# Memory layer: decay of the old states on ScalarE, norm from undivided sums, signed high parts, and states requested in the gates

## Chip, core and metric

One core of one Trainium2 chip. The metric is the device time of one execution in microseconds (us). The engines by their profile names: PE is TensorE (PEld its weight loads), ACT is ScalarE, DVE is VectorE, POOL is GpSimd, SP is SyncE, which issues all DMAs here.

## The reference, cut to what matters

One inference step of a two-layer decoder for a prompt of 256 tokens and for 8 samples of 8 tokens, 320 tokens in all. Layer 0 mixes tokens by a gated MLP, layer 1 by an mLSTM "matrix memory"; a convolutional feed-forward follows each. The change lies in layer 1. For each of 8 heads it computes

```
C, n, m = carry                                  # the old state, 128 x 256 a head and sample
w_inter = exp(inter - m_t);  w_intra = exp(D - m_t)
sc  = (q @ k.T) * w_intra
num = w_inter * (q @ C) + sc @ v
den = w_inter * (q @ n) + sum(sc)
h   = num / maximum(abs(den), exp(-m_t))
decay = exp(bL + m - m_new);  kg = k * g
C_new = decay * C + kg.T @ v
n_new = decay * n + sum(kg)
hn = (h - mean(h)) * rsqrt(var(h) + EPS) * gn_g
y  = (sigmoid(o_pre) * hn) @ w_out
```

Only the samples have an old state; it is an input and its successor an output. Ahead of the layer stands an RMS norm, whose factor 1/sqrt(mean(x²)+EPS) each token's projections are multiplied by.

## The kernel before

**Precision by parts.** Each fp32 weight block of 128x1024 (`raw`) is split into a high part `wh`, rounded (ScalarE, L135), and the rest `wl` (VectorE, L136). A block of 128 outputs is 24 matmuls of 320 columns: `wh` with the high and the low part of the input, `wl` with the high part. Blocks are taken in a fixed list; the load (SyncE) runs 4 chunks ahead into 4 `raw` buffers, the split 1 chunk ahead into 3 pairs of `wh`, `wl`. So a split waits until PE has done with the block three before.

**Order.** PE's instructions keep the order of the program text (`pin`). On the other engines and the queues, a planner in the framework lays out the order from estimated costs, the program's order being the priority; each engine then runs its list strictly in order. Every dependence becomes a semaphore.

**Layer 1** (`layer_b`). `gates` computes, for all heads at once, the gate rows; it begins with the projection `pg`, the norm (`norm_cols`: sums over channels by matmuls with ones, then `ms`, and `rc` by a power on GpSimd; `norm_row`: the same factor as a row `rb`), the first head's q, k, v and output-gate blocks, and the transposes `pt`. Then come heads 1 to 7, each in six weight blocks: q, k (`qk_epi`), two of v (`v_epi`), two of the output gate (`o_epi`), and among them, for that head or the one before:

- `scores`: `pMb` (the head's decays and weights, broadcast to 128 rows), `psc` (q against k), the weights `w` by exp, their product `Pf` and its parts `Ph`, `Pl`, `Pr`, `Ps`, and `dec`, the old states' decay.
- `k_nat`, `v_nat`: transposes `pk`, `pv`, and the parts `kz`, `kgh`, `kgl`, `vh`, `vl`.
- `hand_over`: `inter` (q against the old states `C0`, into `num`), `state_sample` (the new contributions, four tiles `pcs`), `state_out` (C0 = C0·dec + pcs, then its DMA) for two of the four tiles; `close`: `state_out` for the other two, `numer` (`num`), `state_prompt` (`pCp`).
- `stats`: mean and variance of `num`, the normaliser, and `hn`; `finish`: its transposes `phn` and the output's parts `yhb`, `ylb`.

The sums of these helpers lie in five one-bank PSUM buffers (`psa`); the blocks have three of their own (`psm`). The samples' tokens stand twice in a 128-wide tile (`spread`, `twice`), so that one row carries a high part and its twin the low part of the same product; `mk`'s columns are masks for that.

`state_in` requests a head's four `C0` tiles (258 KB each); there are 8 buffers, from the pool `hp`, which opens when the gates' rows are given back.

Of the kernel before, what the change touches and what calls it, by code (L numbers as in the profile page):

```python
# [10 lines left out]
F32 = mybir.dt.float32  # L11
# [5 lines left out]
P = 128  # L17
EPS = 1e-6
TP = 256
NB, NS = 8, 8  # L20
# [17 lines left out]
class Net:  # L38
# [156 lines left out]
    @staticmethod  # L195
    def spread(x):

        return x.rearrange("p (g d s) -> p g d s", g=4, d=2)
# [8 lines left out]

    def norm_cols(self, parts=None, twice=False):
# [5 lines left out]
        if twice:  # L214
            acc2 = self.tp.tile([P, P], F32, tag="acc2", name="acc2", bufs=1)
            nc.vector.tensor_copy(self.spread(acc2), self.twice(self.acc[:, TP:]))
        for t in range(3):
            for i, a in enumerate(parts):
                a_t = acc2 if twice and t == 2 else self.tokens(a, t)
                self.mm(pv[:, t, :], a_t, self.ones[:, :2], i == 0, i == len(parts) - 1)  # L220
# [4 lines left out]
        self.rc, self.rc_twice = rc, twice  # L225

    def norm_row(self):

        nc = self.nc
        dg = self.tp.tile([P, T], F32, tag="sq", name="dg", bufs=2)  # L230
        pb = self.psa.tile([P, 512], F32, tag="pa", name="pb")
        for t in range(2):
            nc.vector.tensor_scalar(dg[:, t * P:(t + 1) * P], self.ident, self.rc[:, t:t + 1], None, op0=MULT)
        if self.rc_twice:
            nc.vector.tensor_scalar(dg[:, TP:].rearrange("p (g s) -> p g s", g=4), self.spread(self.ident)[:, :, 0, :],
                                    self.rc[:, 2:3], None, op0=MULT)
        else:
            nc.vector.tensor_scalar(dg[:, TP:], self.ident[:, 64:], self.rc[:, 2:3], None, op0=MULT)
        self.mm(pb[:, :T], self.ones, dg, True, True)
        rb = self.tp.tile([P, T], F32, tag="rb", name="rb", bufs=1)  # L240
        nc.scalar.copy(rb, pb[:, :T])
        self.rb = rb
# [307 lines left out]
    def layer_b(self):  # L550
# [5 lines left out]
        with ExitStack() as ctx:  # L556
# [4 lines left out]
            nS = lp.tile([P, NH, NB], F32, name="nS")  # L561
            nP = lp.tile([P, NH], F32, name="nP")
# [4 lines left out]
            mk = lp.tile([P, NB + 5], F32, name="mk")  # L567
            mxb = lp.tile([P, 64], F32, name="mxb")
            gm = lp.tile([P, 4, NH], F32, name="gm")
            mo = lp.tile([8, 9], F32, name="mo")  # L570
            mkr = lp.tile([P, NB], F32R, name="mkr")
            pads = []
# [11 lines left out]
            def gates(rp):  # L584
# [126 lines left out]
            def scores(h):  # L711
# [20 lines left out]
                for o in (0, TP):  # L732
# [8 lines left out]

                nc.vector.tensor_scalar(Pr, Pf[:, 384:], mk[:, NB:NB + 1], None, op0=MULT)
                nc.vector.tensor_tensor(spread(Ps)[:, :, 0, :], Pf[:, 384:].rearrange("p (g s) -> p g s", g=4),
                                        Pr.bitcast(F32).rearrange("p (g s) -> p g s", g=4), op=SUB)
                s["P"] = (Ph, Pl, dec)

            def v_nat(h):
# [6 lines left out]
                for t in (2, 0, 1):  # L754
                    dst = dsts[t]
                    sc = self.rc[:, t:t + 1]
                    nc.scalar.activation(vh[:, t, :DV], dst[:, :DV], AF.Copy, scale=sc)
                    nc.vector.scalar_tensor_tensor(vl[:, t, :DV], dst[:, :DV], sc, vh[:, t, :DV].bitcast(F32), op0=MULT, op1=SUB)

            def k_nat(h):  # L760
# [6 lines left out]
                kgl = hp.tile([P, 2, P], F32R, tag="kgl", name="kgl", bufs=1)  # L767
                kr = hp.tile([P, 2, P], F32R, tag="kr", name="kr", bufs=1)
                kz = hp.tile([P, 2, P], F32R, tag="kz", name="kz", bufs=1)
                src = pk[:, 2 * P:3 * P]  # L770

                for i in range(2):
                    nc.vector.tensor_scalar(kr[:, i, :], src, gm[:, 2 + i, h:h + 1], None, op0=MULT)
                    nc.vector.scalar_tensor_tensor(kz[:, i, :], src, gm[:, i, h:h + 1], kr[:, i, :].bitcast(F32), op0=MULT, op1=SUB)
                for t in range(2):
# [6 lines left out]
            def state_in(h):  # L782
                S[h]["C"] = []
                for i in range(4):
                    C0 = hp.tile([P, 2, CW], F32, tag="C0", name="C0", bufs=8)
                    nc.sync.dma_start(C0, I["C0"][h, :, 2 * i:2 * i + 2, :])
                    S[h]["C"].append(C0)

# [20 lines left out]
            def state_out(h, g):  # L809
                s = S[h]  # L810
                dec, C0, pcs = s["P"][2], s["C"][g], s["pcs"][g]
                for u in range(2):
                    b = 2 * g + u
                    nc.vector.scalar_tensor_tensor(C0[:, u, :DV], C0[:, u, :DV], dec[:, b:b + 1], pcs[:, u * DV:(u + 1) * DV],
                                                   op0=MULT, op1=ADD)
                nc.sync.dma_start(O["Cs"][h, :, 2 * g:2 * g + 2, :], C0[:, :, :DV])

# [14 lines left out]
            def stats(h):  # L832
# [13 lines left out]
                nc.vector.tensor_scalar(t1, t1, EPS, None, op0=ADD)  # L846
                sl = hp.tile([P, 3], F32, tag="sl", name="sl", bufs=1)
                nc.gpsimd.tensor_tensor(sl, t1, self.mhalf.to_broadcast([P, 3]), op=ALU.pow)
                nc.vector.tensor_tensor(sl, sl, rd, op=MULT)
                nb = hp.tile([P, 3], F32, tag="nb", name="nb", bufs=1)  # L850
# [4 lines left out]
            def state_prompt(h):  # L855
                s = S[h]
                kgh, kgl, kz = s["kg"]
                dec = s["P"][2]
                pc = self.psa.tile([P, 512], F32, tag="pa", name="pCp")
                for t in range(2):  # L860
                    mm3(pc[:, :CW], kgh[:, t, :], kgl[:, t, :], vh[:, t, :], vl[:, t, :], t == 0, t == 1)
                for i in range(2):
                    mm(pc[:, 264:272], kz[:, i, :], mkr, i == 0, i == 1)
# [78 lines left out]

            state_in(0)
            scores(0)
# [60 lines left out]
            begin(2)  # L1005
            nc.sync.dma_start(O["nP"], nP)
            nc.sync.dma_start(O["nS"], nS)
# [56 lines left out]
def _lay_out(i):  # L1064
# [58 lines left out]
    for h in range(NH):  # L1123
# [3 lines left out]
    tok = s // 32 * 16 + s % 16  # L1127
    low, odd = s // 16 % 2, s // 8 % 2
    a["blk"] = np.concatenate([tok[:, None] // NS == np.arange(NB)[None, :], np.stack(
        [low, 1 - odd, odd, (1 - odd) * low, odd * low], axis=1)], axis=1).astype(f)  # L1130
    a["mxb"] = np.where((tok[:, None] // NS == q[None, :] // NS) & (tok[:, None] <= q[None, :]), f(-1e30), f(1e4))
# [27 lines left out]
```

## Time and profile before

| | |
|---|---|
| median of 3 runs | 970.95 us (970.72 to 971.68) |
| the profiled execution | 970.37 us, of it span 968.6 us |
| busy PE, PEld, DVE, ACT, POOL | 951.8, 922.9, 684.6, 489.8, 75.1 us |
| the memory layer's mixer | 425 to 727 us of the span |
| granted PE clock | 0.996 |

The page gives the busy time of each engine; the waits say for which result an engine stood still, and the timeline lists instructions in order of start, with the number merged in one row behind an x, and in brackets the idle time before the first of them and what ended it. Within a row's name "out<-in" gives tiles. The tile called C is `C0`.

### The profile page before, as it was taken

To read this page: it belongs to the slowest core of one execution; us is meant where nothing else is said; L and a number is where in the kernel's file an instruction comes from. 1 tells how busy PE (TensorE), PEld (TensorE's weight loads), DVE (VectorE), ACT (ScalarE), POOL (GpSimd) and SP (SyncE) were. 2 spreads that over 40 slices of the span, in tenths; PEclk is the share of its full clock that TensorE was granted. 3 is DMA by queue.
4 is the path that set the end of the run, shared out by engine and by line. 5 is a ranking of instruction groups with operands and counts; after the bars stand their busy time and mean duration, and the time that the engine had idled before them with its cause. 6 is when DMAs were issued, how large, how long until landed. Compare 5 with 4: busy or idle time off the path is not lost. (4 is left out here: it accounts for less than half of the span.)

```text
span 968.6 us, 17160 instructions
## 1 busy us (share of the span) xinstructions
PE 951.8 (98%) x6527; PEld 922.9 (95%) x6527; DVE 684.6 (71%) x1333; ACT 489.8 (51%) x851; POOL 75.1 (8%) x248
## 2 busy tenths in 40 slices
PE   9999999999999999999899999999999999999996
PEld 7779999999999999999789999999899999999996
DVE  5757985577777764549889887787787777775442
ACT  6557444444554443447555665464565445454332
POOL 2200000010000000013100001001001000000000
PEclk9999999999999999999999999999999999999998
DMA  7835344434444444453755556544364444445541
GB/s 249 237 130 178 128 138 153 152 131 153 152 153 153 145 152 142 158 174 133 266 182 183 178 181 206 190 152 150 100 216 151 151 145 147 148 149 151 154 123 54
DMA packets 56663, 154.71 MB, mean 160 GB/s; under 512 B 6838, under 2 KB 18486, under 8 KB 56582
## 3 DMA queue, kind: packets, MB, share of 16 engines
q1 hardware_dynamic: 56582, 153.62, 48.4%
q8 instruction: 51, 0.84, 0.4%
q14 instruction: 30, 0.25, 0.1%
HBM read 141.66 MB, written 11.94 MB: 159 GB/s over the span
## 5 line engine op out<-in xcount | busy, mean ns | idle before, releaser
L135 ACT CAST wh<-raw 128x1024 fp32r<-128x1024 f32 (+3 forms) x255 | 257.7, 1011 | 336.6 <-PE pm L47 189.3
L136 DVE TENSOR_TENSOR wl<-raw,wh 128x1024 fp32r<-128x1024 f32 (+3 forms) x255 | 302.0, 1184 | 137.9 <-ACT wh L135 135.6
L47 PE MATMUL pm<-xh,wh 128*128 128x320 f32 x1216 | 379.6, 312 | 0.0
L47 PE MATMUL pm<-xh,wl 128*128 128x320 f32 x1216 | 375.8, 309 | 0.0
L47 PE MATMUL pm<-xl,wh 128*128 128x320 f32 x1216 | 375.7, 309 | 0.0
L47 PEld LDWEIGHTS pm<-xh,wh 128*128 128x128 f32 x1216 | 228.4, 188 | 0.8
L47 PEld LDWEIGHTS pm<-xl,wh 128*128 128x128 f32 x1216 | 228.4, 188 | 0.3
L47 PEld LDWEIGHTS pm<-xh,wl 128*128 128x128 f32 x1216 | 228.2, 188 | 0.0
L47 PE MATMUL pm<-yh_f,wh 128*128 128x320 f32 x352 | 109.0, 310 | 0.0
L47 PE MATMUL pm<-yh_f,wl 128*128 128x320 f32 x352 | 108.5, 308 | 0.0
L47 PE MATMUL pm<-yl_f,wh 128*128 128x320 f32 x352 | 108.5, 308 | 0.0
L47 PEld LDWEIGHTS pm<-yl_f,wh 128*128 128x128 f32 x352 | 66.1, 188 | 0.0
L47 PEld LDWEIGHTS pm<-yh_f,wh 128*128 128x128 f32 x352 | 66.1, 188 | 0.0
L47 PEld LDWEIGHTS pm<-yh_f,wl 128*128 128x128 f32 x352 | 66.1, 188 | 0.0
L472 DVE SCALAR_TENSOR_TENSOR fcv<-fpad,vecs,fcv 128x336 f32<-128x336 f32 x88 | 49.6, 565 | 2.2 <-ACT fcv L470 0.7
L266 DVE TENSOR_TENSOR xT<-pm,xT 128x320 f32<-128x320 f32 x40 | 19.6, 491 | 41.9 <-PE pm L47 41.7
L47 PE MATMUL pm<-yhb,wh 128*128 128x320 f32 x128 | 40.2, 314 | 0.2 <-ACT yhb L891 0.2
L47 PE MATMUL pm<-ylb,wh 128*128 128x320 f32 x128 | 39.6, 309 | 0.4 <-DVE ylb L892 0.4
L47 PE MATMUL pm<-yhb,wl 128*128 128x320 f32 x128 | 39.5, 308 | 0.5 <-DVE wl L136 0.5
L47 PE MATMUL pm<-yh_a,wh 128*128 128x320 f32 x128 | 39.6, 309 | 0.0
L47 PE MATMUL pm<-yh_a,wl 128*128 128x320 f32 x128 | 39.5, 308 | 0.0
L47 PE MATMUL pm<-yl_a,wh 128*128 128x320 f32 x128 | 39.5, 308 | 0.0
(255 smaller groups left out, 1251.3 us busy)
## 6 DMA issues: line engine op xcount, KB each, us to landing
raw<-in_f_up SPq DMA_DIRECT2D x88, 512.0 KB, 3.2
raw<-in_b_win SPq DMA_DIRECT2D x48, 512.0 KB, 3.4
raw<-in_f_dn SPq DMA_DIRECT2D x32, 448.0 KB, 3.2
C<-in_C SPq DMA_DIRECT2D x32, 258.0 KB, 5.1
raw<-in_a_win SPq DMA_DIRECT2D x16, 512.0 KB, 3.2
raw<-in_a_wo SPq DMA_DIRECT2D x16, 512.0 KB, 3.6
raw<-in_f_dn SPq DMA_DIRECT2D x16, 512.0 KB, 3.5
out_Cs<-C SPq DMA_DIRECT2D x32, 256.0 KB, 4.3
```

The costliest lines, as they stand in the source:

```text
L47: self.pin(self.nc.tensor.matmul(out, lhsT, rhs, start=start, stop=stop))
L135: self.last_split = nc.scalar.copy(wh[:, :kn, :], raw[:, :kn, :])
L136: self.last_low = nc.vector.tensor_tensor(wl[:, :kn, :], raw[:, :kn, :], wh[:, :kn, :].bitcast(F32), op=SUB)
L266: self.nc.vector.tensor_tensor(x, ps[:, :T], x, op=ADD)
L472: nc.vector.scalar_tensor_tensor(cv, pd[:, i:i + NC], self.vec(w + i * KF), cv, op0=MULT, op1=ADD)
```

## The change

- `norm_cols` no longer writes the samples' sums out twice before it multiplies them. A new `norm_twice`, behind `norm_row`, makes the doubled copy on ScalarE, and takes one more product and one more power for `v_nat`'s factor `rc2`.
- `dec` is copied by ScalarE, not VectorE, and kept for all heads (`decs`); the update of the normaliser n, two VectorE operations a head, is done once for all heads at the end by GpSimd. ScalarE copies ten columns of `pCp` where it copied one.
- `state_out`: ScalarE multiplies each old state by its decay in place (two instructions a tile), VectorE then adds the tile's `pcs` in one instruction.
- `kz` and `Pr`, `Ps`: the masked rounding is made by ScalarE with a signed mask; VectorE then adds the masked full value (one instruction in place of two).
- `stats`: instead of dividing, the power is taken of var + EPS·d², so three small VectorE steps ahead of it and one behind it go.
- `state_in(0)` moves from behind the gates into them, behind the first q block, and the `C0` buffers move to the layer's own pool `lp`.

```diff
-                self.norm_cols(twice=True)
+                self.norm_cols()
                 p0 = self.block(KD, self.x_rhs)
                 self.norm_row()
+                self.norm_twice()
                 nc.vector.tensor_tensor(zi, gr[:40], self.rb[:40, :], op=MULT)
                 qk_epi(0, 0, p0)
+                state_in(0)
...
+    def norm_twice(self):
+        acc2 = self.tp.tile([P, P], F32, tag="acc2", name="acc2", bufs=1)
+        nc.scalar.copy(self.spread(acc2), self.twice(self.acc[:, TP:]))
+        pc = self.psa.tile([P, 512], F32, tag="pa", name="pc2")
+        self.mm(pc[:, 0:2], acc2, self.ones[:, :2], True, True)
+        ms = self.tp.tile([P, 1], F32, tag="ms2", name="ms2", bufs=1)
+        rc = self.tp.tile([P, 1], F32, tag="rc2", name="rc2", bufs=1)
+        nc.vector.tensor_scalar(ms, pc[:, 0:1], 1.0 / D, EPS, op0=MULT, op1=ADD)
+        nc.gpsimd.tensor_tensor(rc, ms, self.mhalf, op=ALU.pow)
+        self.rc2 = rc
...
-                dec = hp.tile([P, NB], F32, tag="dec", name="dec", bufs=2)
-                nc.vector.tensor_copy(dec, pb[:, 384:392])
+                dec = decs[:, h, :]
+                nc.scalar.copy(dec, pb[:, 384:392])
...
-                nc.vector.tensor_scalar(Pr, Pf[:, 384:], mk[:, NB:NB + 1], None, op0=MULT)
-                nc.vector.tensor_tensor(spread(Ps)[:, :, 0, :], Pf..., Pr..., op=SUB)
+                nc.scalar.activation(Pr, Pf[:, 384:], AF.Copy, scale=mk[:, NB + 5:NB + 6])
+                nc.vector.scalar_tensor_tensor(spread(Ps)[:, :, 0, :], Pf..., mk[:, NB:NB + 1], Pr..., op0=MULT, op1=ADD)
...
                 for i in range(2):
-                    nc.vector.tensor_scalar(kr[:, i, :], src, gm[:, 2 + i, h:h + 1], None, op0=MULT)
-                    nc.vector.scalar_tensor_tensor(kz[:, i, :], src, gm[:, i, h:h + 1], kr[:, i, :].bitcast(F32), op0=MULT, op1=SUB)
+                    nc.scalar.activation(kz[:, i, :], src, AF.Copy, scale=gm[:, i, h:h + 1])
+                    nc.vector.scalar_tensor_tensor(kz[:, i, :], src, gm[:, 2 + i, h:h + 1], kz[:, i, :].bitcast(F32), op0=MULT, op1=ADD)
...
                 for u in range(2):
                     b = 2 * g + u
-                    nc.vector.scalar_tensor_tensor(C0[:, u, :DV], C0[:, u, :DV], dec[:, b:b + 1], pcs[:, u * DV:(u + 1) * DV],
-                                                   op0=MULT, op1=ADD)
+                    nc.scalar.activation(C0[:, u, :DV], C0[:, u, :DV], AF.Copy, scale=dec[:, b:b + 1])
+                nc.vector.tensor_tensor(C0[:, :, :DV], C0[:, :, :DV], pcs.rearrange("p (u v) -> p u v", u=2), op=ADD)
...
                 nc.vector.tensor_tensor(rd, dn, colsT[:, :, 64 + h], op=MAX)
-                nc.vector.reciprocal(rd, rd)
-                t1 = hp.tile([P, 3], F32, tag="t1", name="t1", bufs=1)
-                nc.vector.tensor_tensor(t1, mv[:, :, 1], rd, op=MULT)
-                nc.vector.tensor_tensor(t1, t1, rd, op=MULT)
-                nc.vector.tensor_scalar(t1, t1, EPS, None, op0=ADD)
+                nc.vector.scalar_tensor_tensor(rd, rd, EPS, rd, op0=MULT, op1=MULT)
+                nc.vector.scalar_tensor_tensor(rd, rd, TINY, mv[:, :, 1], op0=MAX, op1=ADD)
                 sl = hp.tile([P, 3], F32, tag="sl", name="sl", bufs=1)
-                nc.gpsimd.tensor_tensor(sl, t1, self.mhalf.to_broadcast([P, 3]), op=ALU.pow)
-                nc.vector.tensor_tensor(sl, sl, rd, op=MULT)
+                nc.gpsimd.tensor_tensor(sl, rd, self.mhalf.to_broadcast([P, 3]), op=ALU.pow)
...
-                nc.scalar.copy(nP[:, h:h + 1], pc[:, DV:DV + 1])
-                nc.vector.tensor_tensor(nS[:, h, :], n0[:, h, :], dec, op=MULT)
-                nc.vector.tensor_tensor(nS[:, h, :], nS[:, h, :], pc[:, 264:272], op=ADD)
+                nc.scalar.copy(nPS[:, h, :], pc[:, DV:DV + 10])
...
+            nc.gpsimd.tensor_tensor(nS, n0, decs, op=MULT)
+            nc.gpsimd.tensor_tensor(nS, nS, nPS[:, :, 2:], op=ADD)
```

More of the change, by code (lines that the diff above doesn't have):

```diff
@@ L18 @@
 EPS = 1e-6
+TINY = 1e-37
 TP = 256
@@ L206, in tokens, with norm_cols @@
         return a[:, (0, P, T - P)[t]:(P, TP, T)[t]]
-    def norm_cols(self, parts=None, twice=False):
+    def norm_cols(self, parts=None):
         nc = self.nc
@@ L213, in norm_cols @@
         pv = pc[:, 0:6].rearrange("p (t e) -> p t e", e=2)
-        if twice:
-            acc2 = self.tp.tile([P, P], F32, tag="acc2", name="acc2", bufs=1)
-            nc.vector.tensor_copy(self.spread(acc2), self.twice(self.acc[:, TP:]))
         for t in range(3):
             for i, a in enumerate(parts):
-                a_t = acc2 if twice and t == 2 else self.tokens(a, t)
-                self.mm(pv[:, t, :], a_t, self.ones[:, :2], i == 0, i == len(parts) - 1)
+                self.mm(pv[:, t, :], self.tokens(a, t), self.ones[:, :2], i == 0, i == len(parts) - 1)
         rc = self.tp.tile([P, 3], F32, tag="rc", name="rc", bufs=2)
@@ L224, in norm_cols @@
         nc.gpsimd.tensor_tensor(rc, ms, self.mhalf.to_broadcast([P, 3]), op=ALU.pow)
-        self.rc, self.rc_twice = rc, twice
+        self.rc = rc
+    def norm_twice(self):
+        nc = self.nc
+        acc2 = self.tp.tile([P, P], F32, tag="acc2", name="acc2", bufs=1)
[7 more added lines that the diff above has]
+        self.rc2 = rc
     def norm_row(self):
@@ L233, in norm_row @@
             nc.vector.tensor_scalar(dg[:, t * P:(t + 1) * P], self.ident, self.rc[:, t:t + 1], None, op0=MULT)
[L234 to L238, printed above, removed]
+        nc.vector.tensor_scalar(dg[:, TP:], self.ident[:, 64:], self.rc[:, 2:3], None, op0=MULT)
         self.mm(pb[:, :T], self.ones, dg, True, True)
@@ L561, in layer_b @@
             nS = lp.tile([P, NH, NB], F32, name="nS")
-            nP = lp.tile([P, NH], F32, name="nP")
             gnh = lp.tile([P, 16], F32, name="gnh")
@@ L566, in layer_b @@
             sel = lp.tile([P, NH, P], F32R, name="sel")
-            mk = lp.tile([P, NB + 5], F32, name="mk")
+            mk = lp.tile([P, NB + 6], F32, name="mk")
             mxb = lp.tile([P, 64], F32, name="mxb")
@@ L570, in layer_b @@
             mo = lp.tile([8, 9], F32, name="mo")
+            decs = lp.tile([P, NH, NB], F32, name="decs")
+            nPS = lp.tile([P, NH, 10], F32, name="nPS")
             mkr = lp.tile([P, NB], F32R, name="mkr")
@@ L755, in v_nat @@
                     dst = dsts[t]
-                    sc = self.rc[:, t:t + 1]
+                    sc = self.rc[:, t:t + 1] if t < 2 else self.rc2
                     nc.scalar.activation(vh[:, t, :DV], dst[:, :DV], AF.Copy, scale=sc)
@@ L767, in k_nat @@
                 kgl = hp.tile([P, 2, P], F32R, tag="kgl", name="kgl", bufs=1)
-                kr = hp.tile([P, 2, P], F32R, tag="kr", name="kr", bufs=1)
                 kz = hp.tile([P, 2, P], F32R, tag="kz", name="kz", bufs=1)
@@ L784, in state_in @@
                 for i in range(4):
-                    C0 = hp.tile([P, 2, CW], F32, tag="C0", name="C0", bufs=8)
+                    C0 = lp.tile([P, 2, CW], F32, tag="C0", name="C0", bufs=8)
                     nc.sync.dma_start(C0, I["C0"][h, :, 2 * i:2 * i + 2, :])
@@ L857, in state_prompt @@
                 kgh, kgl, kz = s["kg"]
-                dec = s["P"][2]
                 pc = self.psa.tile([P, 512], F32, tag="pa", name="pCp")
@@ L941, in close @@
                 state_prompt(h)
-            state_in(0)
             scores(0)
@@ L1128, in _lay_out @@
     low, odd = s // 16 % 2, s // 8 % 2
+    sign = 1 - 2 * low
     a["blk"] = np.concatenate([tok[:, None] // NS == np.arange(NB)[None, :], np.stack(
-        [low, 1 - odd, odd, (1 - odd) * low, odd * low], axis=1)], axis=1).astype(f)
+        [low, (1 - odd) * sign, odd * sign, (1 - odd) * low, odd * low, sign], axis=1)], axis=1).astype(f)
     a["mxb"] = np.where((tok[:, None] // NS == q[None, :] // NS) & (tok[:, None] <= q[None, :]), f(-1e30), f(1e4))
```

9 lines of the change are left out of this document (5 added, 4 removed).

## The prediction

> **What bounds the kernel now.** I read the page first, then the stages, then PE's own waits. All rows in this part and below are of the kernel before.
>
> ```profile
> span 968.6 us, 17160 instructions
> PE 951.8 (98%) x6527; PEld 922.9 (95%) x6527; DVE 684.6 (71%) x1333; ACT 489.8 (51%) x851; POOL 75.1 (8%) x248
> ```
>
> PE is busy for 98% of the span, and the change takes no matmul away. So it can gain only where PE stands still or runs slowly for want of an operand: 16.8 us of the span in all. The table by stage says how much of that lies in the memory layer (columns: stretch, its length, busy us of PE, PEld, DVE, ACT, POOL, granted clock, DMA share, GB/s).
>
> ```profile
> 425.00:727.00 302.00, 294.23 (x2189) 280.91 (x2187) 248.50 (x623) 170.30 (x354) 34.35 (x92) 1.00 0.54 179
> 461.60:490.56 28.96, 24.67 (x192) 20.95 (x191) 25.50 (x70) 15.27 (x37) 4.67 (x7) 1.00 0.66 223
> 490.56:683.00 192.44, 191.37 (x1451) 185.03 (x1452) 158.45 (x406) 106.50 (x227) 17.33 (x51) 1.00 0.53 178
> ```
>
> The layer holds 302.00 − 294.23 = 7.8 us of PE idle time. More than half of it, 4.3 us, lies in the 29 us around heads 0 and 1; heads 2 to 6 (the last row) lose only 1.1 us in 192. VectorE is busy for 82% of the layer and ScalarE for 56%, so the change moves work from the fuller engine to the emptier one, but in the long middle neither holds PE up. The waits of PE name the places (columns: who waited for whom, us in total, times, longest).
>
> ```profile
> PE pcs L47 <- DVE vl L758: 1.4, 1, 1.4
> PE pc L47 <- DVE acc L216: 1.2, 1, 1.2
> PE pk L50 <- ACT w L730: 1.2, 1, 1.2
> ```
>
> ```profile
> PE psc L47 <- ACT kh L274: 1.0, 4, 0.4
> PE phn L50 <- ACT hn L853: 0.8, 1, 0.8
> PE pm L47 <- DVE wl L136: 0.5, 1, 0.5
> PE num L47 <- DMA C<-in_C: 0.5, 1, 0.5
> PE pm L47 <- DVE ylb L892: 0.4, 2, 0.3
> ```
>
> **The change part by part.** The sum is made against the profiled execution, 970.37 us, which is 0.58 us below the median of 970.95.
>
> *Norm.* The timeline of PE at the layer's start, and then at the next norm, which has no doubled sums:
>
> ```profile
> 428.33 0.61 PE L47 MATMUL pc<-ones,acc 128*128 128x2 f32 x4
> 430.19 0.38 PE L47 MATMUL pc<-ones,acc 128*128 128x2 f32 x2 [1.25 <-DVE acc L216]
> 430.43 0.39 PE L47 MATMUL pm<-xh,wh 128*128 128x320 f32 x1
> ```
>
> ```profile
> 726.69 0.72 PE L47 MATMUL pc<-ones,acc 128*128 128x2 f32 x6
> 727.28 0.39 PE L47 MATMUL pm<-xh,wh 128*128 128x320 f32 x1
> ```
>
> Undoubled, the six products pass in 727.28 − 726.69 = 0.59 us, so the block would start at 428.92 and not at 430.43: −1.5. The extra product of `norm_twice` costs a third of 0.59, +0.2, if its copy is done by then; a whole block of matmuls stands between, so I expect no wait. If the planner puts that copy behind the one of the row `rb` on ScalarE, PE waits for both, at most twice this:
>
> ```profile
> L241 ACT COPY rb<-pb 128x320 f32<-128x320 f32 x4 | 1.7, 424 | 0.0
> ```
>
> That would be +0.8. I take −1.5 + 0.2, rounded to −1.2 for a little of that risk; ends −1.5 and −0.4. The new power (`rc2`) takes what POOL's powers take, 0.92 us in a row below, and is first read in `v_nat`, behind the last of the gates' blocks: nothing.
>
> *States requested early.* The first head's 16 products with the old states against the second's:
>
> ```profile
> 462.08 2.82 PE L47 MATMUL num<-C,Qz 128*32 128x258 f32 x16 [0.46 <-DMA C<-in_C]
> 464.82 0.40 PE L47 MATMUL pcs<-vh,kz 32*128 32x256 f32 x4
> ```
>
> ```profile
> 487.80 1.08 PE L47 MATMUL num<-C,Qz 128*32 128x258 f32 x16
> ```
>
> With the tiles there, 2.82 − 1.08 = 1.7 and the wait of 0.46 go: 2.2 us at most. What is late next is the fourth `pcs` buffer, which holds `pk` until its last reader:
>
> ```profile
> 463.05 0.34 DVE L779 SCALAR_TENSOR_TENSOR kgl<-pk,cols,kgh 128x128 fp32r<-128x128 f32 x1
> ```
>
> `pk` is free at 463.4, 1.4 us before `pcs` starts now; VectorE reaches that step earlier by what it is spared, and PE comes earlier by the norm's share. I take half, −1.1 (ends −2.2 and 0). The loads are moved on SP's queue past two or three weight loads; head 1's can follow at once, since all eight buffers are free. The tile's own view gives an issue's length (ns, least, median, most):
>
> ```profile
> L786 SPq DMA_DIRECT2D C<-in_C x32: 327/394/503, 456.9 to 625.4; - x32
> ```
>
> Eight of 0.394 are 3.2 us by which a weight load can come later. Four chunks are loaded ahead, and the chain shows what PE needs for one:
>
> ```profile
> 688.88 3.52 PE pm L47 x24
> ```
>
> So I cost it at nothing. With that cover gone it would be up to 3.2 us, once.
>
> *Old states.* Prices from the groups by form (busy us, mean ns of one):
>
> ```profile
> L814 DVE SCALAR_TENSOR_TENSOR C<-C,dec,pcs 128x256 f32<-128x256 f32 x64 | 26.2, 475 | 0.7 <-PE pcs L47 0.7
> L331 DVE TENSOR_TENSOR vs<-vs,pvs 64x512 f32<-64x512 f32 x4 | 2.8, 692 | 0.1
> L757 ACT ACTIVATE vh<-pv,rc 128x256 fp32r<-128x256 f32 x24 | 11.0, 472 | 3.1 <-DVE vl L758 2.0 <-PE pv L50 1.2
> L773 DVE TENSOR_SCALAR kr<-pk,gm 128x128 fp32r<-128x128 f32 x16 | 5.5, 344 | 0.0
> L742 DVE TENSOR_SCALAR Pr<-Pf,mk 128x64 fp32r<-128x64 f32 x8 | 2.0, 246 | 0.0
> L778 ACT ACTIVATE kgh<-pk,cols 128x128 fp32r<-128x128 f32 x16 | 5.8, 365 | 5.4 <-DVE kz L774 3.3 <-PE pm L47 2.2
> ```
>
> VectorE pays 64·0.475 = 30.4 us now and 32·0.692 = 22.1 after (the sum of two operands of 512 columns, one from PSUM, stands nearest). With 16 `kr` (5.5) and 8 `Pr` (2.0) it sheds 15.8 us, 2 a head, and some seven steps of three to eight columns a head beside. ScalarE's multiplication from SBUF by a column is not in the trace; the nearest row is `vh`, 0.472, of the same size and with the same kind of scale. It gains 64·0.472 + 16·0.365 and the 8 `Pr` at no more than that, 39 us, which makes 209 of 302: no bound. The multiplications wait only for `inter`, not for `pcs`, and this is the gap into which they fall in head 2:
>
> ```profile
> 523.30 1.05 ACT L135 CAST wh<-raw 128x1024 fp32r<-128x1024 f32 x1 [3.67 <-PE pm L47]
> ```
>
> Eight of 0.472 are 3.8 us against 3.67 idle, so the next `wh` is late by 0.1 us, and it is for the block after the next: one block of 3.5 us covers it. If the cover were gone, it would be 0.1 a head.
>
> *Tail and middle.* At the end PE's wait of 0.5 for `wl` follows eight state updates on VectorE; the `ylb` waits of 0.4 follow the same queue; I take −0.8 of these 0.9 (ends −0.9, 0), and −0.5 of the 1.0 for `kh` (ends −1.0, +0.5). The normaliser's two sums on POOL feed nothing but a DMA. Their nearest row is this one:
>
> ```profile
> L848 POOL TENSOR_TENSOR sl<-t,mhalf 128x3 f32<-128x3 f32 x8 | 7.4, 923 | 16.7 <-DVE t L846 16.6
> ```
>
> Two of them make 1.8 us by which SP reaches the weight loads behind that DMA later; the chunks loaded ahead cover it, as above, and without them it is 1.8 once.
>
> *Bank order.* What speaks against the change is in ScalarE's waits:
>
> ```profile
> ACT dn L839 <- DVE bstat L837: 10.4, 17, 1.2
> ```
>
> ```profile
> ACT kgh L778 <- DVE kz L774: 3.3, 3, 1.1
> ```
>
> `dn` needs nothing of `bstat`, nor `kgh` of `kz`; each pair only reads the same PSUM bank, and one engine's reads stand behind the other's. The Trainium skill ("PSUM — Partial Sum Buffer", PSUM bank collisions raise a hardware error) gives the rule: two engines must not touch one bank and quadrant at the same time, not even both to read. By it every added turn is queued, and the sum would be that of the first rival; the trace agrees that turns are kept (the 10.4 us), and not yet that PE pays for them. The change adds such turns: `dec` (ScalarE) ahead of `Qz` and `w` (VectorE) ahead of exp (ScalarE) in `pMb`, and `kz` twice in `pk`. In head 1:
>
> ```profile
> 475.56 0.28 DVE L728 SCALAR_TENSOR_TENSOR w<-pMb,cols,mxb 128x64 f32<-128x64 f32 x1
> 475.75 1.22 DVE L136 TENSOR_TENSOR wl<-raw,wh 128x1024 fp32r<-128x1024 f32 x1
> ```
>
> ```profile
> 476.42 0.76 ACT L730 ACTIVATE w<-pMb,cols 128x256 f32<-128x256 f32 x2
> ```
>
> Now VectorE reads `pMb` at once and ScalarE comes at 476.42. After, `dec` itself takes that place, and if VectorE is then in a `wl`, exp slips by up to 0.3 (`dec`, no longer than the row of `w`) + 1.2 (`wl`) + 0.3 (`w`) = 1.8 us, and PE's wait for `pk` (1.2) with it. Against that, `stats` has four steps fewer and frees `hn` earlier (the 0.8), and VectorE's shorter queue helps `vl` (the 1.4). For head 1 I take −0.6 (ends −2.2 and +1.8), for the same turn in heads 2 to 7 +0.6 (ends 0 and +4).
>
> Sum: −1.2 − 1.1 − 0.8 − 0.5 − 0.6 + 0.6 = −3.6: 966.8 for a profiled execution, 967.3 us as a median.
>
> **Rivals.** *Bank turns decide (slower).* In head 3 the score's bank is given back by `Pf` and PE asks for `pv` here:
>
> ```profile
> 539.79 0.63 DVE L739 SCALAR_TENSOR_TENSOR Pf<-psc,w 128x448 f32<-128x448 f32 x1 [0.17 <-POOL w L733]
> ```
>
> ```profile
> 542.02 0.49 PE L50 MATMUL pv<-ident,vTb 128*128 128x128 f32 x3
> ```
>
> The slack is 542.02 − 540.42 = 1.6 us; a slip of exp by more than that stops PE in each head. At the full 1.8 in head 1 and some 0.6 in each of six heads (0.2 over the slack at `pv`, 0.4 where `kz`'s two turns of 0.34 to 0.37 delay `pk` and `vh`) this is +5.4 against −3.1 from norm, states and tail: about 973.2. That turns are kept the waits of ScalarE show; that PE pays for them no row shows yet. *Next limit close behind.* Norm and tail gain, but at heads 0 and 1 PE meets VectorE's next step in place of the old one: −1.2 − 0.4 and nothing else, 969.4. The full VectorE of that stretch (25.50 of 28.96 us) speaks for it. *All waits go.* The emptier VectorE clears heads 0, 1 and 7 wholly: the good ends, −1.5 − 2.2 − 0.9 − 1.0 − 2.2 = −7.8, or with half of the last three −5.8: 965.2.
>
> **Numbers.** A measurement of this kernel can tell about 0.2%, 1.9 us, from no change. Forecast 0.54, bank turns 0.17, next limit 0.18, all waits 0.11. Faster by over 1.9 us (below 969.0) are the forecast and the last: 0.65; the near limit is "same", 0.18; bank turns slower, 0.17. The range leaves out half of the bank turns and the better half of the last: 964.2 to 971.8.
>
> **What would show it.** Right: one `pc` row of six without a wait, `num` of head 0 in about 1.1 us, no wait of PE for `C`, `C` multiplications on ScalarE in its idle time behind `inter`, VectorE near 232 us in the layer. Wrong: PE waits for `w`, `kh` or `vl` in many heads, or `wh` starts that follow a `C` multiplication rather than PE.

## The result and the profile after

| kernel | median us | runs | lowest to highest |
|---|---|---|---|
| before | 971.32 | 6 | 969.77 to 973.11 |
| changed | 964.59 | 6 | 964.19 to 964.94 |

The ratio is 0.9927, with a 95% interval of 0.9917 to 0.9937: 6.7 us, or 0.7%, faster. (The two profiled executions, 970.37 and 964.48 us, lie 5.9 apart; the rest is scatter between runs.) The prediction's 967.3 had the sign and took a little over half of the size. The page of the changed kernel begins so; PE is busy for 99% of a shorter span.

```profile
span 962.8 us, 17155 instructions
PE 948.8 (99%) x6529; PEld 923.7 (96%) x6529; DVE 672.1 (70%) x1229; ACT 520.4 (54%) x948; POOL 79.5 (8%) x251
```

The table by stage, in the columns of the prediction's: the memory layer, the stretch around heads 0 and 1, and heads 2 to 6.

```profile
425.00:720.00 295.00, 290.01 (x2179) 279.69 (x2178) 236.19 (x518) 200.83 (x450) 38.63 (x92) 1.00 0.57 182
456.60:485.60 29.00, 27.10 (x227) 24.77 (x226) 25.59 (x63) 23.26 (x62) 5.58 (x9) 1.00 0.51 168
485.60:674.00 188.40, 185.92 (x1405) 180.29 (x1405) 148.04 (x320) 124.73 (x286) 19.91 (x49) 1.00 0.56 183
```

The rows are cut at other points than the prediction's, so that their idle times can be compared, but not their lengths. PE's idle time in the layer fell from 7.8 to 5.0 us. Around heads 0 and 1 it fell from 4.3 to 1.9, but in heads 2 to 6 it rose from 1.1 to 2.5. The waits of PE in the layer name what is left:

```profile
PE psc L48 <- DVE khl L281: 2.5, 5, 0.5
PE pk L51 <- ACT hn L858: 1.5, 1, 1.5
PE pm L48 <- DVE wl L137: 0.5, 1, 0.5
PE pcs L48 <- DVE kgl L788: 0.4, 1, 0.4
```

Gone are the waits for `acc`, `C`, `w`, `vl`, `kh`, `ylb` and `yhb`. New is the first line, half a microsecond in each of five heads. The norm and the first head's old states, in PE's timeline:

```profile
427.98 0.83 PE L48 MATMUL pc<-ones,acc 128*128 128x2 f32 x6
...
460.01 1.08 PE L48 MATMUL num<-C,Qz 128*32 128x258 f32 x16
461.02 0.50 PE L48 MATMUL pcs<-vh,kz 32*128 32x256 f32 x3
461.88 0.38 PE L48 MATMUL pcs<-vh,kz 32*128 32x256 f32 x1 [0.36 <-DVE kgl L788]
```

The six products of the norm now form one row without a wait, and the sixteen with the old states take 1.08 us in place of 2.82. What comes late next there is a reader of `pk`. The layer's two ends in the changed kernel, its first product of the gates and the next norm:

```profile
425.24 0.31 PE L48 MATMUL pg<-xh,wl 128*128 128x320 f32 x1
...
720.80 0.72 PE L48 MATMUL pc<-ones,acc 128*128 128x2 f32 x6
```

So the layer takes 295.56 us; before, it began at 425.59 and ended at 726.69, 301.10 us. The difference, 5.54, is nearly all of the span's 5.8. The timelines of PE split it by milestones, each the start of a named row, counted from that first product:

| stretch of PE | before | changed | difference | the prediction's term |
|---|---|---|---|---|
| to `pt` (gates, norm) | 30.10 | 28.91 | −1.19 | norm −1.2 |
| to the last `pcs` of head 0 | 9.59 | 8.07 | −1.52 | states early −1.1 |
| to `num<-vh,Ps` of head 0 | 3.84 | 3.93 | +0.09 | |
| to `num<-vh,Ps` of head 1 | 25.71 | 22.88 | −2.83 | head 1 −0.6 |
| to `pMb` of head 7 | 182.96 | 184.05 | +1.09 | kh −0.5, turns +0.6 |
| to the next norm | 48.90 | 47.72 | −1.18 | tail −0.8 |

### The profile page after: what moved, and what is told of

It reads as the page before. It is cut to its first block, busy times and chain, and to the rows that moved or that the text cites. A ratio compares the mean times of both kernels' runs of the same rounds, so it can differ in the third digit from the quotient of the medians.

```text
span 962.8 us, 17155 instructions
## 1 busy us (share of the span) xinstructions
PE 948.8 (99%) x6529; PEld 923.7 (96%) x6529; DVE 672.1 (70%) x1229; ACT 520.4 (54%) x948; POOL 79.5 (8%) x251
## 4 chain that ended last, share of the span: by engine, by line
PE 85%; issue 10%; DVE 2%; DMA 1%; ACT 0%; SPq 0%; POOL 0%; DVEq 0%; POOLq 0%; ACTq 0%
PE pm L48 74%; PE pv L48 3%; PE num L48 2%; DMA raw<-in_a_wv 1%; PE pvs L48 1%; PE pmix L48 1%; DVE wl L137 1%; PE pCp L48 1%; PE psc L48 1%; PE pcs L48 1%; PE pv L51 1%; PE phn L51 0%; PE pk L51 0%; PE pc L48 0%; PE pg L48 0%
```

## The experiments

All times below are medians; "layer" is the length between the two rows above in the profiled run. It leaves out what differs outside the layer (668.2 to 669.9 us in these runs), but it is one execution of each kernel, so its own scatter is not known; what a difference in it is made of is read from the waits. The kernel before had medians of 971.3 to 971.9 beside these runs.

| run | median us | ratio to before, 95% | layer us |
|---|---|---|---|
| e1 norm back | 966.96 | 0.9940 to 0.9964 | 298.29 |
| e2 states requested late | 965.20 | 0.9924 to 0.9950 | 296.80 |
| e3 divided sums back | 965.71 | 0.9928 to 0.9953 | 296.87 |
| e4 norm and states alone | 966.21 | 0.9933 to 0.9960 | 297.83 |
| e5 hn behind kh | 961.81 | 0.9883 to 0.9912 | 292.54 |
| e6 and early statistics in head 1 | 965.10 | 0.9918 to 0.9942 | 295.25 |
| e7 decay back on VectorE | 971.34 | 0.9983 to 1.0002 | 303.29 |
| e8 dec, kz, Pr back on VectorE | 973.77 | 1.0008 to 1.0027 | 302.95 |
| e9 e6, low parts together | 961.40 | 0.9883 to 0.9914 | 291.77 |
| e10 e7, low parts together | 968.27 | 0.9939 to 0.9971 | 299.75 |
| e11 dec back alone | 967.06 | 0.9942 to 0.9970 | 298.00 |
| e12 e6, wl behind the last vl | 959.78 | 0.9862 to 0.9895 | 291.37 |

**One part undone at a time.** The theory was that each part gives what PE waited for at its place; the rivals, that another limit stood close behind.

*e1:* the doubled sums of the norm are back.

```diff
-                self.norm_cols()
+                self.norm_cols(twice=True)
                 p0 = self.block(KD, self.x_rhs)
                 self.norm_row()
-                self.norm_twice()
```

The copy of the doubled sums is a step of VectorE again, as before.

> The changed kernel with the norm alone put back: the samples' sums are doubled first, on VectorE, and PE's third pair of products waits for them. Theory (each part gives what PE waited at its own place): PE's block behind the norm starts 1.3 us later again, and nothing downstream takes that up, so the time is 1.1 to 1.5 us above the changed kernel's 964.6. Rival (from there to head 1 VectorE sets the pace, so that PE's early start is given back at the next step): at most 0.4 us above.

The layer is 2.73 us longer, more than either theory gave. Two views of this run show why, PE's timeline and the table by stretch (the granted clock is the third column from the end):

```profile
429.62 0.38 PE L48 MATMUL pc<-ones,acc 128*128 128x2 f32 x2 [1.25 <-DVE acc L217]
```

```profile
430.00:433.00 3.00, 3.00 (x13) 3.00 (x13) 0.88 (x5) 1.00 (x1) 0.85 (x1) 0.50 0.92 280
433.00:436.00 3.00, 3.00 (x20) 2.84 (x19) 0.00 (x0) 0.90 (x1) 0.00 (x0) 0.94 0.90 357
```

The wait of 1.25 us came back as the theory says. Behind it the granted clock was 0.50 for 3 us, so that 13 products passed where the changed kernel has 22: another 1.5 us. The kernel before has the same wait of 1.25 us and, in its profiled execution, no such stretch behind it. The Trainium skill ("TensorE: Matmul & The Clock Gate", HAM oscillation) tells of a clock that halves after PE idles for over about 3.4 us; here an idle of 1.25 us did so, and the measurement decides.

*e2:* the states are requested where they were.

```diff
                 qk_epi(0, 0, p0)
-                state_in(0)
...
+            state_in(0)
             scores(0)
```

> The changed kernel with the request of head 0's states put back behind the gates, and the buffers back in the late pool. Theory: head 0's 16 products with the old states take 2.8 us again instead of 1.1, with a wait of PE for C, and the time is 1.0 to 2.2 us above the changed kernel's. Rival (VectorE's last reader of pk, 0.4 us of wait left at that place, is as late as the states were): at most 0.5 us above.

The layer is 1.24 us longer, and PE waits 0.8 for `C`: the theory's lower end by the layer. The median moved by 0.6 alone, nearly what the rival allowed; the wait for `hn` in head 1 shrank at the same time, from 1.5 to 0.7.

*e3:* the statistics divide again.

```diff
-                nc.vector.scalar_tensor_tensor(rd, rd, EPS, rd, op0=MULT, op1=MULT)
-                nc.vector.scalar_tensor_tensor(rd, rd, TINY, mv[:, :, 1], op0=MAX, op1=ADD)
+                nc.vector.reciprocal(rd, rd)
...
+                nc.vector.tensor_tensor(sl, sl, rd, op=MULT)
```

> The changed kernel with the division put back in the statistics: a reciprocal and three small steps ahead of the power, one product behind it. Theory (the chain from the sums to hn sets what PE waits for in head 1): hn of head 0 comes 0.8 to 2 us later, PE's wait for pk grows from 1.5 by as much, and the time is 0.8 to 2 us above the changed kernel's. Rival (the four steps of 0.16 us are too small to matter; it was the weight subtractions queued among them that made hn late, and the shorter VectorE queue that removed those): at most 0.3 us above.

The layer is 1.31 us longer, as the theory had it, but as the sum of two larger things, so that the match is luck. In head 1 PE waits again:

```profile
PE pk L51 <- ACT hn L862: 3.1, 1, 3.1
PE pcs L48 <- DVE vl L768: 1.4, 1, 1.4
```

By `num<-vh,Ps` of head 1 this costs 4.5 us: 2.9 more of waits, and behind the first of them a stretch of 3.41 us at a clock of 0.50. In heads 2 to 6 the waits for `khl` are gone altogether and that gives 3.3 back. So without the shorter statistics chain head 1 is not cleared, and the same chain brings the new wait.

*e4:* norm, early states and the normaliser's later sums alone; statistics, decay, `dec`, `kz` and `Pr` as before.

> Of the change only the norm, the early states and the late update of n: the decay, dec, kz, Pr and the division are VectorE's again. Theory (parts add up): 1.3 + 1.4 of the 6.7 us remain, so about 968.5, some 4 us above the changed kernel; PE waits for pk, phn and vl again in head 1. Rival (the two places that PE waited at longest are the gain, and the relief of VectorE only moves work): within 1.5 us of the changed kernel.

The layer lies 3.27 us under before and 2.27 over the changed kernel; the time lies between theory and rival and decides nothing by itself. The waits do: `w` (1.2), `vl` (1.4, with a stretch at half the clock behind it), `ylb` and `yhb` (0.6) are back, a wait of 1.7 for `bth` came in at `pCp`, and none for `khl`. So the parts do not add up. By the medians the norm, the early states and the later sums bring some 5 of the 6.7 us, twice what the theory gave them, and all the work moved to ScalarE and the shorter statistics only 1.6 more.

**What makes khl late.** In head 2 of the changed kernel, ScalarE, then VectorE, then PE:

```profile
498.20 1.48 ACT L858 ACTIVATE hn<-num,nb,sl 128x256 f32<-128x256 f32 x3 [1.58 <-DVE nb L856]
499.57 0.49 ACT L699 ACTIVATE bth<-bcv 128x344 f32<-128x344 f32 x1
...
500.36 1.08 ACT L136 CAST wh<-raw 128x1024 fp32r<-128x1024 f32 x1
501.50 0.33 ACT L280 CAST kh<-qs 128x128 fp32r<-128x128 f32 x1
```

```profile
500.09 0.42 DVE L701 SCALAR_TENSOR_TENSOR qs<-bth,bcv 128x256 f32<-128x256 f32 x1 [0.82 <-ACT bth L699]
501.47 1.23 DVE L137 TENSOR_TENSOR wl<-raw,wh 128x1024 fp32r<-128x1024 f32 x1 [0.81 <-ACT wh L136]
502.61 0.28 DVE L281 TENSOR_TENSOR khl<-qs,kh 128x128 fp32r<-128x128 f32 x1
```

```profile
502.95 0.38 PE L48 MATMUL psc<-qh,khl 128*128 128x256 f32 x1 [0.51 <-DVE khl L281]
```

`hn`, ready earlier now, is placed ahead of `bth` and ScalarE even waits 1.58 us for it. Behind it `bth`, `qs` and `kh` slip past the cast `wh`, and `khl` past the subtraction `wl`. The kernel before has a milder form of this at the same place, on ScalarE:

```profile
505.19 0.48 ACT L690 ACTIVATE bth<-bcv 128x344 f32<-128x344 f32 x1
506.34 1.48 ACT L853 ACTIVATE hn<-num,nb,sl 128x256 f32<-128x256 f32 x3 [0.67 <-DVE nb L851]
507.85 0.30 ACT L274 CAST kh<-qs 128x128 fp32r<-128x128 f32 x1
```

There `hn` stands behind `bth`, but still ahead of `kh`, and ScalarE waits 0.67 us for it; PE's waits for `kh` follow from that. *e5* changes this order alone; `split` is the cast `kh` of heads 2 to 7, and `normal` holds the three `hn` of the head before:

```diff
+                s["split"] = nc.scalar.copy(hh, qs[:, :n])
...
+                if 0 < h < NH - 1:
+                    with tc.issue_after(S[h + 1]["split"].ins):
+                        normal(h, num, sl, nb)
...
```

> The changed kernel with one order added: in heads 2 to 7 the three normalisations hn of the head before are issued behind the cast kh. Theory (collision on ScalarE): the five new waits of PE for khl come from the shorter statistics chain, which lets hn run ahead of bth, so that qs, kh and khl come late. Then the waits for khl (2.5 us) go, nothing takes their place (phn needs hn some 2 us later than khl is needed), the layer is 2.3 to 2.6 us shorter than in the changed kernel and the time about 962.1. Rival (the subtraction wl ahead of khl on VectorE is what makes it late, whatever ScalarE does): at least 0.4 a head stays, the layer changes by under 0.6 us and the time stays near 964.2. Second rival: hn comes late for phn or holds its banks too long, so that PE waits for hn in five heads: no gain, or a loss of up to 3 us.

The layer is 3.02 us shorter, somewhat beyond the theory's 2.6, and the time 961.81. The waits for `khl` are gone, and `hn` is not late; ScalarE's order in head 2 is now:

```profile
499.67 0.49 ACT L699 ACTIVATE bth<-bcv 128x344 f32<-128x344 f32 x1
501.40 0.30 ACT L711 CAST kh<-qs 128x128 fp32r<-128x128 f32 x1 [0.82 <-DVE qs L701]
501.80 1.47 ACT L866 ACTIVATE hn<-num,nb,sl 128x256 f32<-128x256 f32 x3
```

Each of the five heads is 0.75 us shorter, a quarter of a microsecond more than the wait itself, which no view names. Against that a wait of 0.6 for `vl` came in at `num` of head 7, and the tail is 0.7 us longer; so something did take a little of their place. Both rivals fall; the theory stands.

**What ScalarE's share of the work gives.** *e7:* the old states' update on VectorE again (64 steps of one multiplication and sum).

> The changed kernel with the old states' update on VectorE again, 64 steps of 0.475 us in place of 64 multiplications on ScalarE and 32 sums: VectorE gets 30.4 for 21.9 us. Theory (the tail's and the middle's gains come from VectorE's queue of state updates): the tail's waits for ylb (0.4) and yhb (0.2) come back, the waits for khl grow by some 0.1 a head because VectorE is fuller, the layer is 0.6 to 1.4 us longer, the time 964.8 to 966.0. Rival (VectorE has slack at all these places, the gains came from the norm, the early states and the shorter statistics): the layer changes by under 0.3 us. Rival of the other sign (the multiplications on ScalarE are in the way of the casts): the layer gets 0.3 us or more shorter.

All three were wrong: the layer is 7.73 us longer and the whole gain is gone. None of it lies where the theory sought it: the tail's waits for `ylb` and `yhb` did not come back, and heads 2 to 7 are as long as in the changed kernel to 0.1 us. All of it lies in head 1, in waits of 3.6 for `hn` and 1.4 for `vl` (3.4 us more than in the changed kernel), with the clock at 0.50 at the end of the first and behind each, which makes up most of the other 4.3. VectorE and then PE at the second:

```profile
486.90 0.87 DVE L768 SCALAR_TENSOR_TENSOR vl<-pv,rc,vh 128x256 fp32r<-128x256 f32 x2
487.96 0.49 DVE L875 TENSOR_TENSOR o_b<-pm,rb 128x320 f32<-128x320 f32 x1 [0.18 <-PE pm L48]
488.93 1.23 DVE L137 TENSOR_TENSOR wl<-raw,wh 128x1024 fp32r<-128x1024 f32 x1 [0.48 <-ACT wh L136]
490.07 0.48 DVE L768 SCALAR_TENSOR_TENSOR vl<-pv,rc,vh 128x256 fp32r<-128x256 f32 x1
```

```profile
490.61 0.38 PE L48 MATMUL pcs<-vh,kz 32*128 32x256 f32 x1 [1.37 <-DVE vl L768]
```

The fourth `pcs` starts as the third `vl` ends: it takes the buffer of a `pv` that this `vl` still reads. VectorE is not busy all that time. It does `o_b`, waits 0.48 us for a weight's cast, then does the subtraction `wl`, and only then the `vl` that PE wants: an order in the queue, not an amount of work. The kernel before has these steps in the same order, and that is its wait of 1.36 for `vl`; behind them the changed kernel's:

```profile
486.89 0.87 DVE L758 SCALAR_TENSOR_TENSOR vl<-pv,rc,vh 128x256 fp32r<-128x256 f32 x2
487.90 0.49 DVE L873 TENSOR_TENSOR o_b<-pm,rb 128x320 f32<-128x320 f32 x1
488.88 1.23 DVE L136 TENSOR_TENSOR wl<-raw,wh 128x1024 fp32r<-128x1024 f32 x1 [0.48 <-ACT wh L135]
490.02 0.48 DVE L758 SCALAR_TENSOR_TENSOR vl<-pv,rc,vh 128x256 fp32r<-128x256 f32 x1
```

```profile
482.31 0.87 DVE L768 SCALAR_TENSOR_TENSOR vl<-pv,rc,vh 128x256 fp32r<-128x256 f32 x2
483.10 1.21 DVE L137 TENSOR_TENSOR wl<-raw,wh 128x1024 fp32r<-128x1024 f32 x1
484.23 0.47 DVE L768 SCALAR_TENSOR_TENSOR vl<-pv,rc,vh 128x256 fp32r<-128x256 f32 x1
```

Here too a `wl` stands ahead of the last `vl`, but it runs at once and `o_b` comes behind; the last `vl` ends at 484.70, and PE, whose `pcs` began at 484.41, does not wait.

*e8:* `dec`, `kz`'s first half and `Pr` on VectorE again.

> The changed kernel with the copy of the decays (dec), the first half of kz and Pr on VectorE again: the added turns of ScalarE and VectorE at the banks pMb and pk go, and VectorE does 7.5 us more. Theory (the added turns cost PE nothing, since exp and kz have slack of over a microsecond in every head): the layer changes by less than 0.3 us either way, or is up to 0.6 us longer because VectorE is fuller. Rival (bank turns are paid for in heads 2 to 7, about 0.1 us each, and in head 1): the layer is 0.6 to 1.2 us shorter without them, the time 963.0 to 963.8.

Both were wrong: the layer is 7.39 us longer, and that in the fastest of twelve runs (971.11 us, the median 973.77). The wait for `vl` is there three times (4.1 us in all, one each in heads 2, 3 and 4), each time by the same order of `vl`, `o_b`, `wl`, `vl`; PE waits again for `ylb` and `yhb`, 0.6 us. So the tail's gain hangs on `kz`, `Pr` and `dec`, not on the states' update as the prediction had it; whether by their amount of work or by an order these runs do not tell.

*e11:* `dec` alone back.

> The changed kernel with the copy of the decays (dec) alone on VectorE again, so that no instruction of ScalarE stands ahead of Qz and w at the bank pMb; kz and Pr stay on ScalarE. Theory (that added turn costs PE nothing): the layer changes by less than 0.3 us against the changed kernel, 964.6 us, and the waits for khl stay at 2.5. Rival (the turn is paid for): the layer is 0.4 us or more shorter. Second rival (an order flips, as it must have done with all three copies put back): a wl comes to stand ahead of the last vl or between the small steps of the statistics in some head, PE waits 1.2 to 1.9 us there, and the layer is over 1.2 us longer.

The second rival came true in kind: 2.44 us longer, with waits of 1.3 for `kgl` in head 0 (0.4 in the changed kernel) and of 0.7 for `wl` and 0.5 for `ylb` that the changed kernel doesn't have, while the one for `hn` fell from 1.5 to 0.9. What stands ahead of the late `kgl` are two short steps, `bcv` and `bpad`, and not a `wl`. One copy of eight columns moves steps in the queues and with them whole waits; what its turn at the bank costs by itself can't be read from this run.

**The order itself.** *e10* leaves the update on VectorE as in e7 and changes only the order in which the parts of `v` are written; *e9* does so with e5's order and earlier statistics in head 1, which alone are *e6*: there head 0's statistics are issued one weight block earlier, and the next `wl` behind their third small step.

```diff
                 for t in (2, 0, 1):
...
                     nc.scalar.activation(vh[:, t, :DV], ...)
-                    nc.vector.scalar_tensor_tensor(vl[:, t, :DV], ...)
+                for t in (2, 0, 1):
...
+                    nc.vector.scalar_tensor_tensor(vl[:, t, :DV], ...)
```

> The kernel with the old states' update back on VectorE, and the three vl issued together behind the three vh. Theory (in-order queue: the wait of 1.4 us of pcs for vl in head 1 is a wl ahead of the last vl, not VectorE's amount of work): this wait and the half clock behind it go, the wait of 3.6 us for hn ahead of pk stays, and the layer is 2.3 to 3.1 us shorter than with the update alone put back: 300.2 to 301.0 us, the time about 968.6. Rival (VectorE has too much work in that stretch): the wait for vl stays over 0.9 us, or one for wl takes its place, and the layer shortens by less than 0.8 us.

> As the kernel before in this list, and in head 1 the statistics of head 0 are issued one block earlier, with the next subtraction wl behind their third small step. Theory: the 1.5 us that PE waits for hn ahead of pk in head 1 come from the wl (1.19 us) that stands between the means and the small steps; with it behind them hn ends about 1.1 to 1.5 us earlier, the wait falls to 0 to 0.4 and the layer is 1.1 to 1.5 us shorter than with the order of hn alone: about 960.9. Rival (VectorE is full there, the next limit is close behind): the delayed wl is late for its products, PE waits 0.3 to 1.2 us for wl instead, and the time is that of the order of hn alone, within 0.5 us.

> The kernel with hn behind kh and the earlier statistics in head 1, with one order more: the three high parts vh are written first and the three low parts vl after them, so that no subtraction wl of a weight stands between two vl. Theory (the wait of pcs for vl is one wl of 1.2 us that VectorE's queue holds ahead of the last vl, which keeps the bank of pv): the wait of 1.9 us in head 1 falls to under 0.7, with it the stretch at half the granted clock behind it, and the layer is 3 to 4 us shorter than with the early statistics alone: 291.0 to 292.0 us long, the time about 961. Rival (VectorE is simply full in head 1): another wait of over 1.2 us takes its place there, for wl, vl or ylb, and the time stays at 963 to 965.

In e10 the three `vl` stand in one row and the wait of head 1 is gone, as the theory says. The layer is 3.54 us shorter than in e7, more than expected, but not as cleanly: the wait for `hn` fell to 2.0, and a wait of 1.1 for `vl` came in at head 0, each with the clock at 0.50 behind it.

e6 did what it was made for up to `num<-C` of head 1, which came 1.25 us earlier. Then PE waited for `vl`, and the clock was halved behind it:

```profile
485.73 0.38 PE L48 MATMUL pcs<-vh,kz 32*128 32x256 f32 x1 [1.94 <-DVE vl L774]
```

```profile
488.00:490.00 2.00, 2.00 (x9) 2.00 (x8) 0.94 (x2) 0.00 (x0) 0.00 (x0) 0.50 0.95 320
```

Its time is 3.3 us over e5, worse than the rival had it, and through `vl` and not a late `wl`. In e9 the wait of 1.9 fell to 0.2 and the layer to 291.77, inside the theory's bounds; but head 0, too, was put in another order and lost 0.9 there, so that e9 and e5 can't be told apart by their times. *e12* keeps head 0 as it was; `lst` is the last `vl`, and the next `wl` is issued behind it:

```diff
+                if h == 1:
+                    self.low_behind = lst.ins
...
```

> The changed kernel with hn behind kh, the earlier statistics in head 1, and in head 1 alone the subtraction wl of the next weight behind the last vl; head 0 keeps its order. Theory (in-order queue): in head 1 the waits for hn ahead of pk and for vl ahead of pcs both stay under 0.6 us, head 0 waits no more than the 0.4 for kgl, and the layer is 290.6 to 291.6 us long, 4 to 5 us less than the changed kernel's, the time 960.3 to 961.2. Rival (VectorE is simply full in head 1): a wait of 0.8 us or more for wl, ylb or vl comes in there and the layer stays at 291.8 or more.

The layer is 291.37 us, as the theory had it, and the time 959.78, half a microsecond below its range. In VectorE's queue the last `vl` now stands ahead of the `wl`, and no `pcs` of head 1 waits:

```profile
482.04 0.48 DVE L774 SCALAR_TENSOR_TENSOR vl<-pv,rc,vh 128x256 fp32r<-128x256 f32 x1
482.44 1.21 DVE L142 TENSOR_TENSOR wl<-raw,wh 128x1024 fp32r<-128x1024 f32 x1
```

```profile
482.66 0.39 PE L48 MATMUL pcs<-vh,kz 32*128 32x256 f32 x4
```

This version is the fastest: 0.9879 of the kernel before (0.9862 to 0.9895), and 4.8 us under the changed one, from three changes of order and no change in the work.

## Why the prediction was right, and where it was off

**Norm** (−1.2): right, −1.19, by the way it named. **States requested early** (−1.1): −1.52, between the half it took and its end of −2.2. What is late next is `pk`'s reader `kgl`, as it said, but for 0.36 us only. No weight load came late. e2 gives 1.24 for the same term.

**Tail** (−0.8): −1.18, about right in size and wrong in cause, so that the size is luck. The waits for `ylb` and `yhb` went, the 0.5 for `wl` stayed, and e7 against e8 shows that the relief came from the steps of `kz`, `Pr` and `dec` and not from the eight state updates that the prediction named.

**Head 1** (−0.6): −2.83, beyond the good end of −2.2. This is the largest mis-sized term. The step weighed a slip of exp against small gains "beside it" for `hn` (0.8) and `vl` (1.4). Both went entirely; only the wait ahead of `pk` stayed, 1.5 for `hn` in place of 1.2 for `w`. The step took a wait as something that shrinks in proportion to the work shed. For `vl` the runs show it as all or nothing: e3, e4 and e7 put things back on VectorE, and each brings its wait back whole, 1.37 us (e8 in other heads), with `o_b` and a `wl` ahead of the last `vl`. For `hn` they do not: its wait ahead of `pk` was 0.7 (e2), 0.9 (e11), 1.9 (e8), 3.1 (e3) and 3.6 (e7). (`stats` has three VectorE steps fewer a head, not four: two of them ahead of the power, one behind it.)

**Middle** (−0.5): +1.09 with the term for the turns, the wrong sign. The waits for `kh` (1.0) went, but waits for `khl` (2.5) took their place at the next products of the same `psc`; by the traces both come from ScalarE waiting for `hn` with `kh` queued behind it. The failed step is the one that counted the shorter statistics only as a gain: `hn`, freed earlier, took ScalarE ahead of `bth` in five heads, at 0.5 us of waiting each (e3 and e5). That is the mechanism of the rival "next limit close behind", at another place than heads 0 and 1, where the rival put it.

**Bank turns** (+0.6, and a rival at 0.17): the added turn is in the groups of the changed kernel, where `Qz` waits for `decs`:

```profile
L733 DVE SCALAR_TENSOR_TENSOR Qz<-qs,pMb 128x64 f32<-128x64 f32 x8 | 1.7, 213 | 0.9 <-ACT decs L731 0.9
```

It is 0.9 us in all, and no wait of PE names it: none for `w` is left. So the rival's slip of 1.8 in head 1 didn't happen, nor that of 0.6 in the others. What the turns cost without a change of order stays open, since e8 and e11 both changed the order.

**Prices.** The multiplication on ScalarE and the sum on VectorE, by group:

```profile
L823 ACT ACTIVATE C<-C,decs 128x256 f32<-128x256 f32 x64 | 27.3, 503 | 0.0
L824 DVE TENSOR_TENSOR C<-C,pcs 128x512 f32<-128x512 f32 x32 | 21.6, 685 | 1.8
```

They took 503 and 685 ns for the 472 and 692 assumed. In head 1 the multiplications fall into the idle time behind `inter`, and the next `wh` starts on PE's account, not theirs. VectorE is busy for 236 us in the layer, not 232: the prediction took 64 times the mean length, 30.4 us, for the old update, where its row has 26.2 us of busy time (neighbours overlap). So the update sheds 26.2 − 21.6 = 4.6 us and not 8.3.

Together: −1.2 − 1.5 + 0.1 − 2.8 + 1.1 − 1.2 = −5.5 in the layer against −3.6. The time came out near the 965.2 of the rival by which all waits go, but not by that way: a new wait of 2.5 us was paid, and head 1 gave more than even that rival had. That the time lies in the forecast's range owes something to luck: head 1 gave 2.2 us more than its term, and the middle took 1.0 more.

## What to carry to other kernels

Where each engine works through its queue in order, as here, what PE waits for is what stands ahead of the wanted step, and work shed elsewhere may give nothing until it changes that. In the runs that put a part back, the wait for `vl` was there whole, 1.4 us, or not at all. So the parts of a change do not add up: put back one at a time, the norm, the states, the division, the update and `dec`, `kz` and `Pr` cost some 20 us by the medians (e1, e2, e3, e7, e8), where together they had gained 6.7. Read, at each wait, which instruction stood ahead of the releaser on its engine, and whether that one was waiting itself. When a chain is made shorter, ask what its result will now be placed ahead of: the five new waits of this change were cured by an order alone, and three orders gave 4.8 us where the whole change had given 6.7.

## What the runs showed of the hardware

The granted clock fell to 0.50 behind short waits of PE: of 1.25 us (e1), 3.10 (e3), 1.37 (e4), 1.94 (e6), 3.60 and 1.37 (e7), 1.13 and 2.03 (e10). Behind others it stayed at 1.00: 1.25 and 1.36 (before), 1.54 (changed), 1.37 (e3), 1.69 (e4), 1.53 (e5), 1.91 and three of 1.37 (e8), 1.11 (e9), 1.27 (e11). So length alone doesn't decide, up to about 2 us; in e1 the halving doubled the price of the wait. Each such stretch lasted 3.41 us; only e7's first lasted twice that, from 1.7 us before its wait ended:

```profile
475.00:481.83 6.83, 5.13 (x20) 5.13 (x21) 2.17 (x7) 3.99 (x11) 1.33 (x3) 0.50 0.60 225
481.83:492.06 10.23, 8.86 (x82) 7.75 (x81) 7.55 (x15) 5.08 (x10) 0.00 (x0) 1.00 0.25 78
492.06:495.47 3.41, 3.41 (x15) 3.41 (x14) 2.44 (x7) 0.00 (x0) 0.00 (x0) 0.50 0.90 313
```

The second begins 17.06 us after the first, five times 3.41; in e10 (464.08 and 477.73) it is 13.65 us, four times. So in these two runs the clock changed on a fixed grid of 3.41 us. The same page of the Trainium skill ("TensorE: Matmul & The Clock Gate", Part 1) says that the clock follows PE's activity in windows of some 3.4 us that run freely; the lengths and distances here agree. That would make equal waits differ by how they fall against the windows, as 1.13 in e10 and 1.11 in e9 do at the same product, but no run here moves a wait against such a window, so this is not shown. Executions of one kernel differ as well: the twelve runs of e7 had mean granted clocks of 0.995 down to 0.991 and took 969.1 to 972.6 us. A price that contains such a stretch, as e1's 2.73 us, holds for the profiled execution.
